# Stick-breaking attention: logits in three 64-row products a head on the two halves of the array, first weights made by VectorE and ScalarE

## The chip, the cores and the metric

The kernel runs on one core of one Trainium2 chip, as one launch. The metric is the device time in microseconds, the median of several executions. One further execution was profiled; all rows quoted here come from its trace.

## The reference, cut to what matters

A two-layer decoder trunk over 1040 tokens (16 learned ones ahead of 1024) and 1024 channels: a Mamba-2 layer with a convolutional FFN, then an attention layer with a second FFN. The change lies in the attention alone, and in the last step ahead of it.

```python
q = (_rmsnorm(h, sb_norm[j]) @ sb_w_q[j]).reshape(b, L, SB_HEADS, SB_HEAD_DIM)   # 16 heads of 64
k_shared, v_shared = split(_rmsnorm(h, kv_norm) @ w_kv)
# for each block of query rows t and key columns s:
logits = jnp.einsum('bthd,bshd->bhts', q, k).astype(jnp.float32) * scale
visible = s_idx < t_idx
log_keep = jnp.where(visible, jax.nn.log_sigmoid(-logits), 0.0)
later = lax.cumsum(log_keep, axis=3, reverse=True) - log_keep
log_w = jnp.where(visible, jax.nn.log_sigmoid(logits) + later, -jnp.inf)
out = jnp.einsum('bhts,bshd->bthd', jnp.exp(log_w), v)
```

All of it is float32, and the logits have to be nearly that exact.

## The kernel before, in words

Activations lie with channels on the partitions and tokens along the free side. Float32 products are made from a high and a low part: `mm3` (L160 to L165) gives high x high, high x low and low x high as three products at the fast rate of the rounded type (`F32R`). The normalised stream `u` is such a pair of tiles for each of eight channel blocks (`KD`); the factor of the RMSNorm for each token is not multiplied in, but lies in `u[KD]` and is applied to what comes out of the products. Tokens are projected in three stretches `TT` of 348, 348 and 344.

At the end of the first FFN, `norm` (L238) is called for each stretch `j`: `parts` splits `h` into `u` (ScalarE copies the high part, VectorE subtracts the low one, L262 and L263), `square_sum` adds the squares (L229, L233, L235), and `rstd` (L190) sums them over the partitions with a product by ones (L196) and makes the factor (L199 to L204). This part is ordered by the scheduler.

The attention (L1414) is in program order on TensorE, VectorE, ScalarE and GpSimd. It works on eight pairs of heads. For each pair, `load` (L1237) fetches the weights of k, q and v (SyncE, L1241), scales them with the norm's gain and splits them into `wh` and `wl`. For the first pair GpSimd scales (L1249) and subtracts (L1254) whole 128x1024 tiles with ScalarE copying between (L1253); for the others VectorE does both in halves (L1260, L1268) with ScalarE's copies between (L1266).

`half` (L1272) does half of one projection (12 products, tile `pj`). When it is whole, a key goes to `key` (L1295), a query to `stack` (L1306). The logits of one head need q.k over 64 channels in the three parts high x high, high x low, low x high. Before, two products of 128 rows do this: the two tiles of `me.ks` and the query's tiles are stacked, so that the 64 rows of the head hold one part and the other 64 rows another. [...] VectorE multiplies the key by the token factor first (L1289), ScalarE takes the high part (L1300, L1313), VectorE the low one (L1301, L1317).

A pair then runs through 18 steps `(i, jj)`: i is one of nine blocks of 116 query rows (112 the last) and jj a stretch of keys, the diagonal one first. In each step, in this order on TensorE: `weigh` (L1351) makes the logits of both heads (L1363, four products into two banks of one tile, 116, 232 or 344 to 348 columns wide), `place` turns projected values (L1330), `half` does its 12 products for the rest of this pair (the first eight steps) or for the next pair (the other ten; the last pair has none there), in every other block `values` (L1394) multiplies weights and values with the two heads in the two halves of the array's columns (L1403), and `turn` (L1379) turns the weights of an earlier step (L1388). ScalarE takes two sigmoids of the logits (L1365), GpSimd masks the diagonal (L1370), VectorE scans (L1374) and multiplies (L1375).

Ahead of the first step stand, in this order, the loads of k, q and v, the projections k, q for the first stretch and k, q for the second (96 products), and `token_factors` (L1337), which turns the token factors of all three stretches (L1345).

Of the kernel before, what the change touches and what calls it, by code (L numbers as in the profile page):

```python
# [8 lines left out]
F32 = mybir.dt.float32  # L9
F32R = mybir.dt.float32r  # L10
AF = mybir.ActivationFunctionType
ALU = mybir.AluOpType

P = 128
D = 1024
KD = D // P
# [7 lines left out]
TW = 352  # L24
QW = 1056
HALO = 4
# [42 lines left out]
class Trunk:  # L69
# [168 lines left out]
    def norm(self, h, j, u):  # L238

        s0, n = TT[j]  # L240
        if u is None:
            u = [(self.Q("uh", F32R), self.Q("ul", F32R)) for _ in range(KD)] + [self.rp.tile([P, QW], F32, tag="r", name=self.nm("r"))]
        rows = [h[k][:, s0 : s0 + n] for k in range(KD)]
        for k in range(KD):
            self.parts(rows[k], u[k], s0, n, None, self.nc.vector)
        self.rstd(self.square_sum(rows, n, D), n, D, u[KD][:, HALO + s0 : HALO + s0 + n], j == 0)
        return u

    def scaled_project(self, w, u, j, q=None, bank=None):
# [977 lines left out]
    def heads(self, u, p, pool):  # L1227


        nc, a = self.nc, self.a  # L1230

        class Pair:
            def __init__(me):
                me.w, me.qd, me.ps = {}, {}, {}
                me.late, me.old = [], []

            def load(me, kind):  # L1237

                src, gain = {"k": (a["w_kv"][p], "kv_norm"), "q": (a["w_q"][p], "sb_norm"), "v": (a["w_kv"][PAIRS + p], "kv_norm")}[kind]
                w32 = self.wp.tile([P, 1024], F32, tag="w32", name=self.nm("w32"))  # L1240
                nc.sync.dma_start(w32, src)  # L1241
                if kind == "k":
                    me.ks = [self.Q("k", F32R), self.Q("k", F32R)]
                elif kind == "v":
                    me.v = pool.tile([P, 9, P], F32, tag="v", name=self.nm("v"), bufs=2)

                def scale():
                    v = w32.rearrange("p (k c) -> p k c", k=KD)
                    nc.gpsimd.tensor_tensor(v, v, self.par(gain, 0, KD).unsqueeze(2).to_broadcast([P, KD, P]), op=ALU.mult)  # L1249

                def parts():
                    me.w[kind] = wh, wl = [self.wp.tile([P, 1024], F32R, tag=t, name=self.nm(t)) for t in ("wh", "wl")]
                    nc.scalar.activation(wh, w32, AF.Copy)  # L1253
                    nc.gpsimd.tensor_tensor(wl, w32, wh.bitcast(F32), op=ALU.subtract)  # L1254

                def scale_halves():
                    for x in range(2):
                        v = w32[:, D // 2 * x : D // 2 * (x + 1)].rearrange("p (k c) -> p k c", c=P)
                        g = self.par(gain, KD // 2 * x, KD // 2).unsqueeze(2).to_broadcast([P, KD // 2, P])
                        nc.vector.tensor_tensor(v, v, g, op=ALU.mult)  # L1260

                def part_halves():
                    me.w[kind] = [self.wp.tile([P, 1024], F32R, tag=t, name=self.nm(t)) for t in ("wh", "wl")]
                    halves = [[t[:, D // 2 * x : D // 2 * (x + 1)] for t in (w32, *me.w[kind])] for x in range(2)]
                    for w, wh, _ in halves:
                        nc.scalar.activation(wh, w, AF.Copy)  # L1266
                    for w, wh, wl in halves:
                        nc.vector.tensor_tensor(wl, w, wh.bitcast(F32), op=ALU.subtract)  # L1268

                return [scale_halves, part_halves] if p else [scale, parts]  # L1270

            def half(me, kind, j, h):  # L1272

                s0, n = TT[j]
                if h == 0:
                    me.ps[kind, j] = self.pj.tile([P, 512], F32, tag="mm", name=self.nm("pj"), bufs=2)
                ps = me.ps[kind, j]
                o, e = HALO + s0, HALO + s0 + n
                wh, wl = me.w[kind]
                for k in range(4 * h, 4 * h + 4):  # L1280
                    self.mm3(ps[:, :n], wh[:, k * P : k * P + P], wl[:, k * P : k * P + P], u[k][0][:, o:e], u[k][1][:, o:e], k == 0, k == KD - 1)
                if h == 0:
                    return []
                del me.ps[kind, j]
                if kind == "q":
                    return [lambda: me.stack(j, ps)]
                t = self.tmp(kind)
                if kind == "k":
                    nc.vector.tensor_tensor(t[:, :n], ps[:, :n], u[KD][:, o:e], op=ALU.mult)  # L1289
                    return [lambda: me.key(j, t)]  # L1290
                nc.scalar.activation(t[:, :n], ps[:, :n], AF.Copy)
                me.late.append((j, t))
                return []

            def key(me, j, t):  # L1295

                s0, n = TT[j]
                c = slice(s0, s0 + n)
                lo, x, y = self.tmp("klo"), *me.ks
                nc.scalar.activation(x[:, c], t[:, :n], AF.Copy)  # L1300
                nc.vector.tensor_tensor(lo[:, :n].bitcast(F32R), t[:, :n], x[:, c].bitcast(F32), op=ALU.subtract)  # L1301
                nc.sync.dma_start(y[64:, c].bitcast(F32), x[64:, c].bitcast(F32))
                nc.sync.dma_start(y[:64, c].bitcast(F32), lo[64:, :n])
                nc.sync.dma_start(x[64:, c].bitcast(F32), lo[:64, :n])

            def stack(me, j, q):  # L1306

                n = TT[j][1]
                out = []
                for a, own in enumerate((slice(0, 64), slice(64, P))):  # L1310
                    t = self.Q("qs", F32R) if j else pool.tile([P, 2 * TW], F32R, tag="qs", name=self.nm("qs"), bufs=2)
                    hi, lo = (t[:, i * TW : i * TW + n] for i in range(2))
                    nc.scalar.activation(hi[own], q[own, :n], AF.Copy)  # L1313
                    out.append((t, hi, lo))
                for a, own in enumerate((slice(0, 64), slice(64, P))):
                    t, hi, lo = out[a]
                    nc.vector.tensor_tensor(lo[own], q[own, :n], hi[own].bitcast(F32), op=ALU.subtract)  # L1317
                    both = t[:, : 2 * TW].bitcast(F32).rearrange("p (i c) -> p i c", i=2)[:, :, :n]
                    nc.sync.dma_start(both[64 - 64 * a : P - 64 * a], both[own])
                me.qd[j] = [x[1:] for x in out]  # L1320

            def place(me):

                todo, me.old, me.late = me.old, me.late, []
                for j, t in todo:
                    v = me.v
                    pv = self.sm("pv")
                    for i in range(3):
                        m = CH[3 * j + i][1]
                        nc.tensor.transpose(pv[:m, i * P : i * P + P], t[:, i * CB : i * CB + m], self.ident)  # L1330
                    for x, y, m in ((0, 3, CB),) if j < 2 else ((0, 2, CB), (2, 3, CH[8][1])):
                        nc.vector.tensor_tensor(v[:m, 3 * j + x : 3 * j + y], pv[:m, x * P : y * P].rearrange("p (c d) -> p c d", d=P),
                                                self.rt[0][:m, 3 * j + x : 3 * j + y].unsqueeze(2).to_broadcast([m, y - x, P]), op=ALU.mult)

        return Pair()
# [15 lines left out]
    def weigh(self, i, jj, qd, ks, prev, pool, ps):  # L1351

        nc = self.nc
        t0, nt = CH[i]
        j, c0 = i // 3, (i % 3) * CB
        s0 = TT[jj][0]
        m = min(TT[jj][1], t0 + nt - s0)
        kp = pool.tile([P, 2, TW], F32, tag="kp", name=self.nm("kp"), bufs=3)
        bt = pool.tile([P, 2, TW], F32, tag="bt", name=self.nm("bt"), bufs=4)
        nc.gpsimd.memset(kp[:nt, :, m : m + 1], 1.0)  # L1360
        for a in range(2):
            for x, part in enumerate(qd[a]):
                nc.tensor.matmul(ps[:nt, a, :m], part[:, c0 : c0 + nt], ks[a][:, s0 : s0 + m], start=x == 0, stop=x == 1)  # L1363
        for t, r in ((kp, self.rt[2]), (bt, self.rt[1])):
            nc.scalar.activation(t[:nt, :, :m], ps[:nt, :, :m], AF.Sigmoid, scale=r[:nt, i : i + 1])  # L1365
        if jj == j:

            for t, fill in ((kp, 1.0), (bt, 0.0)):
                own = t[:nt, :, c0 : c0 + nt]
# [44 lines left out]
    def attention(self, u, pool):  # L1414
# [11 lines left out]
        both = lambda p: p.tile([P, 2, 512], F32, tag="lg2", name=self.nm("lg"))  # L1426
# [20 lines left out]
        for kind, j in (("k", 0), ("q", 0), ("k", 1), ("q", 1)):  # L1447
            for h in range(2):
                for f in first.half(kind, j, h):
                    f()  # L1450
        self.token_factors(u[KD], pool)
        for p in range(PAIRS):
            prev = None
            for n, (i, jj) in enumerate(steps):
# [6 lines left out]
                ps = both(more if p + 1 == PAIRS and n > 8 and n % 2 else self.lp)  # L1461
# [198 lines left out]
```

## Time and profile before

| | |
|---|---|
| median of 3 runs | 2900.92 us (2900.5 to 2902.97) |
| the profiled execution's own time | 2900.43 us |
| its span in the trace | 2898.6 us |
| TensorE busy over the span | 2827.6 us (98%) |
| VectorE, ScalarE, GpSimd | 2111.8, 1642.1 and 674.6 us |
| granted TensorE clock, mean | 0.994 |
| the steps of the attention in the span | from about 1577 to 2093 us |

A row of a timeline reads: start in us from the span's start, its length, the engine (PE is TensorE's product, PEld its weight load, DVE VectorE, ACT ScalarE, POOL GpSimd, SPq SyncE's queue), line, operation, output<-inputs, rows*columns of the array, output's shape, and how many instructions were merged; in brackets the idle time before it and what ended it. A row of a group gives busy time, mean ns, and idle time before. Products are pipelined, so their lengths overlap; their pace is seen from their starts.

### The profile page before, as it was taken

How to read it: one execution, taken by the hardware profiler on the slowest of the kernel's cores; microseconds unless marked ns; L12 is line 12 of the kernel's file. 1: busy time of each engine (PE TensorE's matmuls, PEld its weight loads, DVE VectorE, ACT ScalarE, POOL GpSimd, SP SyncE). 2: the span in 40 equal slices, each digit the busy share in tenths (PEclk: the TensorE clock that was granted, in tenths of full speed). 3: DMA queues.
4: the chain of work that ended last, by engine and by line, in shares of the span. 5: the costliest groups of instructions: out<-in, count | busy, mean ns of one | idle time of the engine just before them, and what ended most of it. 6: DMA issues, size and time to landing. Idle time of an engine off the chain costs nothing.

```text
span 2898.6 us, 55788 instructions
## 1 busy us (share of the span) xinstructions
PE 2827.6 (98%) x21808; PEld 2704.6 (93%) x21808; DVE 2111.8 (73%) x3860; ACT 1642.1 (57%) x3202; POOL 674.6 (23%) x668
## 2 busy tenths in 40 slices
PE   8999999999999999999999999999999999999998
PEld 5989898988999999999998999999898999999888
DVE  5685868776578656568986888888869655657895
ACT  5576667773245555555334777677736555555442
POOL 0000000000004666660002111121101766662000
PEclk9999999999999999999999999999999999999999
DMA  6233333323221222226142222222341222225331
GB/s 168 78 112 86 117 93 108 113 67 136 86 98 66 74 82 76 80 88 214 57 136 77 61 63 63 67 67 56 117 169 46 88 81 81 76 79 189 109 109 59
DMA packets 134135, 274.76 MB, mean 95 GB/s; under 512 B 16464, under 2 KB 68304, under 8 KB 133872
## 3 DMA queue, kind: packets, MB, share of 16 engines
q1 hardware_dynamic: 128560, 260.26, 28.3%
q10 hardware_dynamic: 4048, 6.36, 0.6%
q0 software_dynamic: 1264, 4.57, 0.4%
q8 instruction: 172, 2.82, 0.4%
q14 instruction: 91, 0.75, 0.1%
HBM read 203.02 MB, written 53.21 MB: 88 GB/s over the span
## 4 chain that ended last, share of the span: by engine, by line
PE 70%; DVE 5%; issue 2%; ACT 1%; DMA 1%; POOL 0%; DVEq 0%; ACTq 0%; SPq 0%; POOLq 0%
PE p L163 10%; PE p L165 10%; PE p L164 10%; PE acc L165 8%; PE acc L164 8%; PE acc L163 8%; PE pj L163 3%; PE pj L165 3%; PE pj L164 3%; PE po L1403 2%; PE lg L1363 2%; PE wT L1388 2%; DVE kp L1374 1%; DVE bl L875 1%; DVE ft L879 0%
## 5 line engine op out<-in xcount | busy, mean ns | idle before, releaser
L163 PE MATMUL pj<-uh,wh 128*128 128x348 f32 (+2 forms) x1536 | 502.0, 327 | 10.5 <-DVE xbc L286 9.7
L164 PE MATMUL pj<-ul,wh 128*128 128x348 f32 (+2 forms) x1536 | 494.9, 322 | 0.0
L165 PE MATMUL pj<-uh,wl 128*128 128x348 f32 (+2 forms) x1536 | 493.2, 321 | 0.0
L163 PE MATMUL p<-bh,fh 128*128 128x262 f32 (+1 forms) x1408 | 401.0, 285 | 9.2 <-DVE p L999 4.7
L164 PE MATMUL p<-bl,fh 128*128 128x262 f32 (+1 forms) x1408 | 400.5, 285 | 0.2
L165 PE MATMUL p<-bh,fl 128*128 128x262 f32 (+1 forms) x1408 | 399.3, 284 | 0.0
L163 PEld LDWEIGHTS pj<-uh,wh 128*128 128x128 f32 x1536 | 288.9, 188 | 17.0 <-issue 12.9
L163 PE MATMUL p<-bh,wh 128*128 128x262 f32 (+1 forms) x1056 | 302.3, 286 | 1.2 <-ACT bh L874 1.0
L164 PE MATMUL p<-bl,wh 128*128 128x262 f32 (+1 forms) x1056 | 301.2, 285 | 1.0 <-DVE bl L875 1.0
L165 PE MATMUL p<-bh,wl 128*128 128x262 f32 (+1 forms) x1056 | 302.1, 286 | 0.0
L164 PEld LDWEIGHTS pj<-ul,wh 128*128 128x128 f32 x1536 | 289.4, 188 | 1.5 <-issue 0.6
L165 PEld LDWEIGHTS pj<-uh,wl 128*128 128x128 f32 x1536 | 289.0, 188 | 0.7 <-issue 0.2
L163 PEld LDWEIGHTS p<-bh,fh 128*128 128x128 f32 x1408 | 268.1, 190 | 10.9 <-DVE p L999 5.1
L286 DVE SCALAR_TENSOR_TENSOR c<-p,params,c 128x260 f32<-128x260 f32 (+1 forms) x440 | 207.8, 480 | 91.8 <-ACT c L282 89.8
L164 PEld LDWEIGHTS p<-bl,fh 128*128 128x128 f32 x1408 | 267.6, 190 | 0.8 <-DVE bl L875 0.6
L165 PEld LDWEIGHTS p<-bh,fl 128*128 128x128 f32 x1408 | 266.9, 190 | 0.3
L930 POOL TENSOR_TENSOR fl<-x,fh 128x1024 fp32r<-128x1024 f32 x80 | 192.2, 2403 | 251.7 <-ACT fh L929 251.7
L999 DVE TENSOR_TENSOR p<-p,ft 128x262 f32<-128x262 f32 (+1 forms) x176 | 76.3, 435 | 214.8 <-ACT ft L996 124.4
L164 PE MATMUL acc<-gl,wh 128*128 128x260 f32 (+1 forms) x672 | 211.3, 320 | 0.4 <-DVE gl L1097 0.4
L165 PE MATMUL acc<-gh,wl 128*128 128x260 f32 (+1 forms) x672 | 208.7, 320 | 0.0
L164 PEld LDWEIGHTS p<-bl,wh 128*128 128x128 f32 x1056 | 202.6, 192 | 1.6 <-DVE bl L875 1.6
L163 PEld LDWEIGHTS p<-bh,wh 128*128 128x128 f32 x1056 | 202.5, 192 | 1.7 <-ACT bh L874 1.2
(316 smaller groups left out, 7521.7 us busy)
## 6 DMA issues: line engine op xcount, KB each, us to landing
w<-in_w_up SPq DMA_DIRECT2D x92, 512.0 KB
w<-in_w_down SPq DMA_DIRECT2D x44, 512.0 KB
w<-in_w_in SPq DMA_DIRECT2D x40, 512.0 KB
E<-ea_d SPq DMA_DIRECT2D x32, 464.0 KB
D<-acs_d SPq DMA_DIRECT2D x32, 420.5 KB
g<-c SPq DMA_DIRECT2D x88, 130.0 KB
g<-c SPq DMA_DIRECT2D x88, 128.0 KB
b<-g SPq DMA_DIRECT2D x16, 520.0 KB
```

The source lines that it names most:

```text
L163: mm(out, wh, uh, start=first, stop=False, skip_group_check=joins)
L164: mm(out, wh, ul, start=False, stop=False, skip_group_check=joins)
L165: mm(out, wl, uh, start=False, stop=last, skip_group_check=joins)
L286: nc.vector.scalar_tensor_tensor(to, ps[:, o + i : o + i + n], wcol(i), out, op0=ALU.mult, op1=ALU.add)
L875: tt(hl[1], x, hl[0].bitcast(F32), op=ALU.subtract)
L930: (self.nc.vector if b < 2 else self.nc.gpsimd).tensor_tensor(lo[:, :n], t, hi[:, :n].bitcast(F32), op=ALU.subtract)
L999: add = lambda o, x, y: tt(o[:, :N], x[:, :N], y[:, :N], op=ALU.add)
L1363: nc.tensor.matmul(ps[:nt, a, :m], part[:, c0 : c0 + nt], ks[a][:, s0 : s0 + m], start=x == 0, stop=x == 1)
L1374: nc.vector.tensor_tensor_scan(rev, rev, self.one[:nt].to_broadcast([nt, m + 1]), init, ALU.mult, ALU.mult)
L1388: nc.tensor.transpose(pt[:ns, x * CB : x * CB + nt], bt[a][:nt, x * CB : x * CB + ns], self.ident[:nt, :nt])
L1403: nc.tensor.matmul(po[64 * a : 64 * a + 64, w], v[: CH[c][1], c, 64 * a : 64 * a + 64], wt[a][: CH[c][1], c, :nt], start=x == 0, stop=x == ...
```

## The change

The two heads of a pair lie on partitions 0 to 63 and 64 to 127, in the query as in the key, as the projection leaves them. After the change they stay there: `key` and `stack` make one high and one low tile over all 128 partitions, without copies, and `weigh` makes three products of 64 rows for each head, the heads in turn, so that consecutive products use the upper and the lower 64 rows of the array and write different banks.

Besides, the first pair's weights are made as the other pairs' are, by VectorE and ScalarE in halves, and `norm` keeps the last stretch's `rstd` back; the attention calls it behind the first key and query projections.

```diff
 def norm(self, h, j, u):
-        self.rstd(self.square_sum(rows, n, D), n, D, u[KD][:, HALO + s0 : HALO + s0 + n], j == 0)
+        sums = self.square_sum(rows, n, D)
+        factor = lambda: self.rstd(sums, n, D, u[KD][:, HALO + s0 : HALO + s0 + n], j == 0)
+        if j < 2:
+            factor()
+        else:
+            self.last_factor = factor
 def load(me, kind):
-                def scale():
-                    ...
-                    nc.gpsimd.tensor_tensor(v, v, self.par(gain, 0, KD).unsqueeze(2).to_broadcast([P, KD, P]), op=ALU.mult)
-                def parts():
-                    ...
-                    nc.scalar.activation(wh, w32, AF.Copy)
-                    nc.gpsimd.tensor_tensor(wl, w32, wh.bitcast(F32), op=ALU.subtract)
-                return [scale_halves, part_halves] if p else [scale, parts]
+                return [scale_halves, part_halves]
 def key(me, j, t):
-                lo, x, y = self.tmp("klo"), *me.ks
-                nc.scalar.activation(x[:, c], t[:, :n], AF.Copy)
-                nc.vector.tensor_tensor(lo[:, :n].bitcast(F32R), t[:, :n], x[:, c].bitcast(F32), op=ALU.subtract)
-                nc.sync.dma_start(y[64:, c].bitcast(F32), x[64:, c].bitcast(F32))
-                nc.sync.dma_start(y[:64, c].bitcast(F32), lo[64:, :n])
-                nc.sync.dma_start(x[64:, c].bitcast(F32), lo[:64, :n])
+                hi, lo = (x[:, s0 : s0 + n] for x in me.ks)
+                nc.scalar.activation(hi, t[:, :n], AF.Copy)
+                nc.vector.tensor_tensor(lo, t[:, :n], hi.bitcast(F32), op=ALU.subtract)
 def stack(me, j, q):
-                for a, own in enumerate((slice(0, 64), slice(64, P))):
-                    t = self.Q("qs", F32R) if j else pool.tile([P, 2 * TW], F32R, tag="qs", name=self.nm("qs"), bufs=2)
-                    ...
-                    nc.scalar.activation(hi[own], q[own, :n], AF.Copy)
-                for a, own in enumerate((slice(0, 64), slice(64, P))):
-                    ...
-                    nc.vector.tensor_tensor(lo[own], q[own, :n], hi[own].bitcast(F32), op=ALU.subtract)
-                    nc.sync.dma_start(both[64 - 64 * a : P - 64 * a], both[own])
-                me.qd[j] = [x[1:] for x in out]
+                t = self.Q("qs", F32R)
+                hi, lo = (t[:, i * TW : i * TW + n] for i in range(2))
+                nc.scalar.activation(hi, q[:, :n], AF.Copy)
+                nc.vector.tensor_tensor(lo, q[:, :n], hi.bitcast(F32), op=ALU.subtract)
+                me.qd[j] = hi, lo
 def weigh(self, i, jj, qd, ks, prev, pool, ps):
-        for a in range(2):
-            for x, part in enumerate(qd[a]):
-                nc.tensor.matmul(ps[:nt, a, :m], part[:, c0 : c0 + nt], ks[a][:, s0 : s0 + m], start=x == 0, stop=x == 1)
+        for x, (q, k) in enumerate(((qd[0], ks[0]), (qd[0], ks[1]), (qd[1], ks[0]))):
+            for a in range(2):
+                own = slice(64 * a, 64 * a + 64)
+                nc.tensor.matmul(ps[:nt, a, :m], q[own, c0 : c0 + nt], k[own, s0 : s0 + m], start=x == 0, stop=x == 2)
 def attention(self, u, pool):
+            if (kind, j) == ("q", 0):
+                self.last_factor()
```

More of the change, by code (lines that the diff above doesn't have):

```diff
@@ L1245, in load @@
                     me.v = pool.tile([P, 9, P], F32, tag="v", name=self.nm("v"), bufs=2)
-                def scale():
-                    v = w32.rearrange("p (k c) -> p k c", k=KD)
-                    nc.gpsimd.tensor_tensor(v, v, self.par(gain, 0, KD).unsqueeze(2).to_broadcast([P, KD, P]), op=ALU.mult)
-                def parts():
-                    me.w[kind] = wh, wl = [self.wp.tile([P, 1024], F32R, tag=t, name=self.nm(t)) for t in ("wh", "wl")]
-                    nc.scalar.activation(wh, w32, AF.Copy)
-                    nc.gpsimd.tensor_tensor(wl, w32, wh.bitcast(F32), op=ALU.subtract)
                 def scale_halves():
@@ L1297, in key @@
                 s0, n = TT[j]
-                c = slice(s0, s0 + n)
-                lo, x, y = self.tmp("klo"), *me.ks
-                nc.scalar.activation(x[:, c], t[:, :n], AF.Copy)
-                nc.vector.tensor_tensor(lo[:, :n].bitcast(F32R), t[:, :n], x[:, c].bitcast(F32), op=ALU.subtract)
-                nc.sync.dma_start(y[64:, c].bitcast(F32), x[64:, c].bitcast(F32))
-                nc.sync.dma_start(y[:64, c].bitcast(F32), lo[64:, :n])
-                nc.sync.dma_start(x[64:, c].bitcast(F32), lo[:64, :n])
+                hi, lo = (x[:, s0 : s0 + n] for x in me.ks)
+                nc.scalar.activation(hi, t[:, :n], AF.Copy)
+                nc.vector.tensor_tensor(lo, t[:, :n], hi.bitcast(F32), op=ALU.subtract)
             def stack(me, j, q):
                 n = TT[j][1]
-                out = []
-                for a, own in enumerate((slice(0, 64), slice(64, P))):
-                    t = self.Q("qs", F32R) if j else pool.tile([P, 2 * TW], F32R, tag="qs", name=self.nm("qs"), bufs=2)
-                    hi, lo = (t[:, i * TW : i * TW + n] for i in range(2))
-                    nc.scalar.activation(hi[own], q[own, :n], AF.Copy)
-                    out.append((t, hi, lo))
-                for a, own in enumerate((slice(0, 64), slice(64, P))):
-                    t, hi, lo = out[a]
-                    nc.vector.tensor_tensor(lo[own], q[own, :n], hi[own].bitcast(F32), op=ALU.subtract)
-                    both = t[:, : 2 * TW].bitcast(F32).rearrange("p (i c) -> p i c", i=2)[:, :, :n]
-                    nc.sync.dma_start(both[64 - 64 * a : P - 64 * a], both[own])
-                me.qd[j] = [x[1:] for x in out]
+                t = self.Q("qs", F32R)
[3 more added lines that the diff above has]
+                me.qd[j] = hi, lo
             def place(me):
```

## The prediction

> **What bounds the kernel now.** I read the page first, then busy time by stretches, then the chain of waits, and last the timeline of the two places that the diff touches: the seam before the attention, and one logits group in it.
>
> ```profile
> PE 2827.6 (98%) x21808; PEld 2704.6 (93%) x21808; DVE 2111.8 (73%) x3860; ACT 1642.1 (57%) x3202; POOL 674.6 (23%) x668
> PE 70%; DVE 5%; issue 2%; ACT 1%; DMA 1%; POOL 0%; DVEq 0%; ACTq 0%; SPq 0%; POOLq 0%
> ```
>
> TensorE is nearly always busy and holds 70% of the chain. By stretches (columns: PE, weight loads, DVE, ACT, POOL, then granted clock):
>
> ```profile
> 1554.00:1560.00 6.00, 1.87 (x6) 1.18 (x5) 4.21 (x2) 0.53 (x3) 3.92 (x2) 0.62 0.35 117
> 1618.00:1684.00 66.00, 65.80 (x572) 62.77 (x571) 55.76 (x83) 46.30 (x103) 13.03 (x37) 1.00 0.23 63
> 2057.00:2096.00 39.00, 32.12 (x339) 27.87 (x336) 35.17 (x48) 32.58 (x74) 7.39 (x18) 1.00 0.47 159
> ...
> 1687.41 2.33 PE po L1403 x44
> 1752.96 2.33 PE po L1403 x44
> ```
>
> The last two rows are the same values group (L1403) of neighbouring pairs in the chain: a pair takes 65.55 us, and in it TensorE is busy 65.80 of 66. So in pairs 0 to 6 every ns that a logits group takes on TensorE is a ns of the kernel. Only the last pair, which has no next pair's projections, leaves TensorE about 7 us of slack (32.12 of 39). The seam (1554 to 1560) is the one hole: 1.87 busy of 6, clock down to 0.62.
>
> **Part 1: the logits.** Before, a head's group is two products of 128 rows, four a step for both heads; after, three products of 64 rows a head, six a step. The steps by columns of the moving side:
>
> ```profile
> L1363 PE MATMUL lg<-k,qs x576: 255/321/419, 1576.6 to 2083.6; 128*116 128x348 f32 x80, 128*116 128x116 f32 x48, 128*116 128x232 f32 x32, 128*112 128x344 f32 x16
> L1363 PE MATMUL lg<-k,qs 128*116 128x232 f32 x96 | 16.0, 288 | 0.0
> L1363 PE MATMUL lg<-k,qs 128*116 128x116 f32 x96 | 14.4, 272 | 0.0
> ...
> 1755.40 0.86 PE L1363 MATMUL lg<-k,qs 128*116 128x348 f32 x4
> 1756.10 0.33 PE L163 MATMUL pj<-uh,wh 128*128 128x348 f32 x1
> 1756.27 0.32 PE L164 MATMUL pj<-ul,wh 128*128 128x348 f32 x1
> ...
> 1777.56 0.67 PE L1363 MATMUL lg<-k,qs 128*116 128x232 f32 x4
> 1778.07 0.49 PE L1330 MATMUL pv<-ident,v 128*116 128x128 f32 x3
> ...
> 1783.91 0.60 PE L1363 MATMUL lg<-k,qs 128*116 128x116 f32 x4
> 1784.34 0.52 PE L1330 MATMUL pv<-ident,v 128*116 128x128 f32 x3
> ```
>
> 576 products are 144 steps: 24 with 116 columns, 24 with 232, the other 96 with 344 or 348 (12 of 18 in a pair). Starts, not durations, give the pace, since products overlap: 348 columns come every 0.16 us (1756.10 to 1756.27), so a wide group is 0.64. From its first start to the next product it is 0.70; the middle group is 0.51 and the narrow one 0.43, so these are 0.45 (0.11 each) and 0.37 (0.09 each).
>
> Does a 64-row product run beside the one in the other half? No row here shows it for rows. The nearest is the values product, which alternates between two halves of the columns:
>
> ```profile
> 1642.77 3.13 PE po L1403 x60
> 1636.49 0.60 PE wT L1388 x6
> ```
>
> 60 of them with 116 columns take 3.13 us, 0.052 each; the transposes, 116 columns too but over the whole array, take 0.60/6 = 0.10. So halves do run two at a time, weight loads included. Bounds for six half products: three rounds (0.48, 0.33, 0.27) to six in a row (0.96, 0.66, 0.54). I take three rounds, with the values row. That saves 0.16, 0.11 and 0.09 a group.
>
> What stands against it is the change of the array's shape, twice a step: the transposes ahead of the group and the projections behind it use all 128 rows. The trace has such a visit, a 16-row transpose among whole products, and one to column halves:
>
> ```profile
> 56.65 0.32 PE L165 MATMUL pj<-uh,wl 128*128 128x352 f32 x1
> 56.90 0.13 PEld L323 LDWEIGHTS xT<-ident,x 16*128 16x128 f32 x1 [0.22 <-issue]
> 57.06 0.43 PE L163 MATMUL pj<-uh,wh 128*128 128x352 f32 x1
> 57.16 0.19 PEld L164 LDWEIGHTS pj<-ul,wh 128*128 128x128 f32 x1
> 57.32 0.32 PE L164 MATMUL pj<-ul,wh 128*128 128x352 f32 x1
> ...
> 1773.62 0.32 PE L165 MATMUL pj<-uh,wl 128*128 128x348 f32 x1
> 1773.87 0.62 PE L1403 MATMUL po<-wt,v 116*64 116x116 f32 x8
> ```
>
> Products of this size follow each other at 0.16, yet the 16-row weights start loading only 0.25 later (56.90), and so does the values group (1773.62 to 1773.87): 0.09 of emptying, and the weight load, hidden otherwise, now stands alone (0.10: next load at 57.16 after 57.06). On the way back the same: the whole product's start at 57.06 is 0.26 ahead of the next instead of 0.16, again 0.10 of bare load, behind another 0.05 to 0.09 of emptying. A visit costs 0.09 + 0.10 + 0.08 + 0.10 = 0.37 us. The Trainium skill, "TensorEngine Tiling (Array Packing)", section "Key Properties", says that changing the tiling mode drains TensorE while changing the tile does not; that puts 64-row halves with these rows, which no run here shows for 64 rows. By the doubling that its "Theoretical Speedup" table gives alone, the gaining rival below would be the forecast.
>
> So a group gets longer by 0.37 less the saving: 0.21 wide, 0.26 middle, 0.28 narrow. It counts where TensorE sets the pace: pairs 0 to 6 and the first eight steps of the last pair (they still carry projections; 4 wide, 2 middle, 2 narrow), that is 88 wide, 23 middle, 23 narrow: 18.5 + 6.0 + 6.4 = 30.9 us.
>
> Off that go waits that swallow part of it:
>
> ```profile
>   ACT bt L1365: 1.4, 7
>   PEld pj L163: 2.2, 7
> ...
> L1313 ACT ACTIVATE qs<-pj x48: 439/452/458, 1568.3 to 2054.0; 64x348 fp32r<-64x348 f32 x32, 64x344 fp32r<-64x344 f32 x16
> L1317 DVE TENSOR_TENSOR qs<-pj,qs x48: 500/516/524, 1570.1 to 2056.3; 64x348 fp32r<-64x348 f32 x32, 64x344 fp32r<-64x344 f32 x16
> ```
>
> The first row: before seven logits groups TensorE already waits for ACT to free the bank, 1.4 us together. The second: seven times the projections wait for DVE to finish a query split, 2.2 us; that split shrinks from two instructions of 0.516 to one (all 128 partitions at once), ACT's from two of 0.452 to one, so I take 1.5 of the 2.2 as gone. 30.9 - 1.4 - 1.5 = 28.0. In the last pair's ten later steps TensorE's slack of 7 us covers most of 10 x 0.25; I put 0.5 (0 to 2.5 if the longer group delays the sigmoids). DVE and ACT lose 24 instructions each, some 12 and 10 us in all, and SyncE loses, by the code, six query and nine key copies a pair: no gain, because DVE (55.76 of 66) and ACT (46.30) have slack, and no logits group waits for a copy.
>
> The Trainium skill, "TensorE: Matmul & The Clock Gate", section "Measured speedup vs the span model", gives 3.07 for four 32-row tiles, not 4, which no run here shows. As an estimate, rounds longer by 4/3.07 would add about 0.14 us a wide group and put the kernel near 2940.
>
> **Part 2: the seam.**
>
> ```profile
> 1552.13 0.51 DVE L263 TENSOR_TENSOR ul<-h,uh 128x344 fp32r<-128x344 f32 x1
> 1552.31 1.06 ACT L1253 ACTIVATE wh<-w 128x1024 fp32r<-128x1024 f32 x1
> 1553.44 2.35 POOL L1254 TENSOR_TENSOR wl<-w,wh 128x1024 fp32r<-128x1024 f32 x1 [66.53 <-ACT wh L1253]
> 1554.08 2.09 DVE L263 TENSOR_TENSOR ul<-h,uh 128x344 fp32r<-128x344 f32 x1 [0.56 <-ACT uh L262]
> 1556.09 2.20 DVE L235 TENSOR_TENSOR sq<-sq,sq 128x344 f32<-128x344 f32 x1
> 1558.35 1.52 PE L196 MATMUL ms<-sq,ones 128*128 128x344 f32 x2 [4.13 <-DVE sq L235]
> 1560.24 0.49 PE L164 MATMUL pj<-ul,wh 128*128 128x348 f32 x1
> 1562.42 0.32 PE L163 MATMUL pj<-uh,wh 128*128 128x348 f32 x1
> L1260 DVE TENSOR_TENSOR w<-w,params x42: 681/683/687, 1600.0 to 2013.4; 128x512 f32<-128x512 f32 x42
> L1268 DVE TENSOR_TENSOR wl<-w,wh x42: 678/866/897, 1604.6 to 2017.5; 128x512 fp32r<-128x512 f32 x42
> ```
>
> While GpSimd splits the first weights, the same DVE subtraction takes 2.09 instead of 0.51; TensorE waits 4.13 for the square sum, does the sum's two products, and resumes in a slow clock until 1562.42, the thirteenth projection product. After, GpSimd does none of this, and the last factor comes behind the first 48 products. TensorE then needs DVE's first low half: ACT ends at 1553.37, plus one 0.87, plus perhaps a 0.51 ahead of it, so about 1554.6; the thirteenth product is at about 1556.2. Off the 6.2 gained go the two sums, done later (0.7, an estimate: their 1.52 roughly halved at full clock), and DVE's queue: from 1553.4, six subtractions at 0.87, four scalings at 0.68 (the first two fit earlier) and two old ones, 8.9 us, then the first key's 0.52 before its bank is free at about 1562.9, where TensorE asks for it at 1562.5. Another 0.4 to 0.7. I take -4.5: bounds -6 (nothing late) and -1 (DVE's first scaling falls behind the square sums, and TensorE waits for two more instructions and ACT). The factor's own ACT and DVE steps lie beside the second key and query (48 products, 7.7 us) ahead of the transposes that need them; without that cover they would cost about 3 us. The sums' products wait in TensorE's queue for DVE's square sum, with the second key behind them; the sum is ready at about 1556, TensorE comes to it near 1562.
>
> **Sum.** 28.0 + 0.5 - 4.5 = +24.0 on the profiled 2900.43, which is 0.5 under the median of 2900.92: 2924. Faster or slower here means by more than 0.2% (5.8 us), about what a measurement of this kernel can tell.
>
> **The rivals.**
> (1) *Halves without emptying.* If whole products and 64-row halves follow each other freely, groups get shorter: 88 x 0.16 + 23 x 0.11 + 23 x 0.09 = 18.7, with 1.5 and 4.5 on top: 2876. For it: the values product shows the doubling. Against: its own entry at 1773.87 shows the price. A visit under about 0.19 us decides for this side (134 visits against 18.7 + 1.5 + 4.5).
> (2) *Halves compute together, but their weights load in turn*, 0.10 each: six loads bound the group, +0.39 wide and about +0.54 else: 57.8 after the bank wait, so 2953. Against: the values pace of 0.052 a product with its load.
> (3) *Halves do not run together at all*, the change not doing what it says: +0.69, +0.59, +0.55, less the same waits, 2981. Against: the same row, though it is for columns.
>
> **How the numbers follow.** The forecast 0.70 (own range 2912 to 2936: 0.03 us either way on 134 visits, and the seam's bounds); rival 1 0.10, as both entries speak against it; rival 2 0.09; rival 3 0.07; a visit at about half price, 2896 to 2907, 0.04. The range 2906 to 2955 holds the first and rival 2. Slower 0.86, same 0.03, faster 0.11.
>
> **What would show it.** Right: logits products in pairs a few ns apart, three rounds a group; the first logits load about 0.19 us behind the last transpose's start (0.10 pace, 0.09 emptying), a bare projection load behind the group; a pair of about 69.3 us; at the seam no 4 us hole, no slow clock, DVE subtractions at 0.5 to 0.9. Wrong: a pair under 65 us (rival 1), loads 0.10 apart (2), or 0.16 between halves (3).

## The result, and the profile after

| | median us | against the kernel before (ratio, 95% interval) |
|---|---|---|
| before | 2902.36 (6 runs) | |
| changed | 2917.51 (6 runs) | 1.0055 (1.0044 to 1.0066) |

The change costs 15 us. The profiled execution of the changed kernel took 2919.47, 2 over its median. Its first projection product comes 1.83 us later than in the profile before. Of that, 1.34 stands already ahead of the FFN's last product, where nothing is changed, so times of one place are compared from a start inside that place, not from the span's start. The rest is the change's own, 0.48 by the waits in these rows: VectorE's first weight subtraction (L1264) now stands ahead of the addition that the first projection waits for (the first row is the kernel before, the others the changed one):

```profile
1553.67 0.40 PE L163 MATMUL pj<-uh,wh 128*128 128x348 f32 x1 [0.61 <-DVE h L398]
...
1554.33 0.68 DVE L1264 TENSOR_TENSOR wl<-w,wh 128x512 fp32r<-128x512 f32 x1
1554.93 0.42 DVE L403 TENSOR_TENSOR h<-h,acc 128x260 f32<-128x260 f32 x1
1555.50 0.40 PE L163 MATMUL pj<-uh,wh 128*128 128x348 f32 x1 [1.09 <-DVE h L403]
```

The page, then the stretches (columns as before), then the same values group of neighbouring pairs in the chain:

```profile
PE 2855.0 (98%) x22096; PEld 2691.0 (92%) x22096; DVE 2103.1 (72%) x3848; ACT 1638.6 (56%) x3181; POOL 655.9 (22%) x662
PE 73%; DVE 4%; DMA 1%; ACT 1%; issue 0%; DVEq 0%; ACTq 0%; POOL 0%; SPq 0%
...
1556.00:1562.00 6.00, 6.00 (x40) 6.00 (x39) 5.85 (x11) 2.62 (x5) 0.00 (x0) 1.00 0.57 199
1690.00:1759.00 69.00, 69.00 (x614) 60.71 (x611) 54.61 (x81) 45.48 (x98) 12.07 (x36) 1.00 0.09 32
...
1688.11 2.33 PE po L1389 x44
1756.62 2.33 PE po L1389 x44
```

A pair takes 68.51 us instead of 65.55. TensorE is now busy in all 69 us of it by its records. The hole ahead of the attention is gone (6.00 of 6, full clock). One wide logits group (L1349) among its neighbours, in the timeline:

```profile
1693.37 0.76 PE L1374 MATMUL wT<-ident,bt 116*116 116x116 f32 x6
1694.06 0.73 PE L1349 MATMUL lg<-k,qs 64*116 64x348 f32 x6
1694.73 0.43 PE L163 MATMUL pj<-uh,wh 128*128 128x348 f32 x1
1694.99 0.32 PE L164 MATMUL pj<-ul,wh 128*128 128x348 f32 x1
```

Six products take 0.73 us by their record. In the trace they come in three rounds of two: the two products of a round start 3 ns apart, and so do their weight loads; the second round starts 0.25 behind the first, whose weights load alone, and the third 0.16 behind the second. The six transposes' record ends at 1694.13 and one is 0.26 long, so the last starts at 1693.87, and the logits at 1694.06: 0.19, of which 0.10 is the transposes' pace. Behind the group the projections' first product is 0.26 ahead of the second (0.16 otherwise): the second product's weight load is not hidden. From the last transpose to that second product it is 1.12 us. Before, it was 0.90 (1755.37 to 1756.27), and the logits (1755.40) started 0.03 behind the last transpose, the second of this row:

```profile
1755.22 0.41 PE L1388 MATMUL wT<-ident,bt 116*116 116x116 f32 x2
```

### The profile page after: what moved, and what is told of

The parts are those of the page before. It is cut to its first block, busy times and chain, and to the rows that moved or that the text cites. A ratio compares the mean times of both kernels' runs of the same rounds, so it can differ in the third digit from the quotient of the medians.

```text
span 2917.8 us, 55934 instructions
## 1 busy us (share of the span) xinstructions
PE 2855.0 (98%) x22096; PEld 2691.0 (92%) x22096; DVE 2103.1 (72%) x3848; ACT 1638.6 (56%) x3181; POOL 655.9 (22%) x662
## 4 chain that ended last, share of the span: by engine, by line
PE 73%; DVE 4%; DMA 1%; ACT 1%; issue 0%; DVEq 0%; ACTq 0%; POOL 0%; SPq 0%
PE p L164 10%; PE p L163 10%; PE p L165 10%; PE acc L165 8%; PE acc L164 8%; PE acc L163 8%; PE pj L163 4%; PE pj L165 3%; PE pj L164 3%; PE lg L1349 3%; PE po L1389 3%; PE wT L1374 3%; DVE bl L880 1%; DVE ft L884 0%; DVE c L291 0%
## 5 line engine op out<-in xcount | busy, mean ns | idle before, releaser
L163 PE MATMUL pj<-uh,wh 128*128 128x348 f32 (+2 forms) x1536 | 512.4, 334 | 10.9 <-DVE xbc L291 9.8
L163 PE MATMUL acc<-gh,wh 128*128 128x260 f32 (+1 forms) x672 | 204.3, 320 | 0.0
```

Source lines behind the costliest of these rows:

```text
L163: mm(out, wh, uh, start=first, stop=False, skip_group_check=joins)
```

## The experiments

**The seam alone**, with the logits of before:

```diff
 (before)
-                return [scale_halves, part_halves] if p else [scale, parts]
+                return [scale_halves, part_halves]
-        self.rstd(self.square_sum(rows, n, D), n, D, u[KD][...], j == 0)
+        ...   # kept back for the last stretch, called behind the first key and query, as in the change
```

> The kernel before with the seam alone changed: first weights by VectorE and ScalarE in halves, the last factor behind the first key and query; logits as before (128 rows, stacked by copies). Theory: the hole of 4 us ahead of the attention closes, and TensorE reaches the transposes of the token factors about 6 us sooner after its first projection product (22.0 us in the kernel before, 15.9 in the changed one); all of it counts, as TensorE sets the pace behind it: -5 to -6 us, near 2897. Rival: the time is given back in the first steps, where ScalarE loads a table and the scans start: no change within 2 us.

2897.49 us, ratio 0.9982 (0.9973 to 0.9991): the gain is 5.1 us and stays.

**The logits alone**, with the seam of before:

```diff
 (changed)
-                return [scale_halves, part_halves]
+                return [scale_halves, part_halves] if p else [scale, parts]
-            if (kind, j) == ("q", 0):
-                self.last_factor()
```

> The changed kernel with the old seam (GpSimd makes the first weights, the last factor ahead of the projections): the logits part alone. Theory: +3.0 us a pair as in the changed kernel's trace, +21 in seven pairs and up to 1.7 in the last, so near 2923 to 2925, and the parts add up: seam alone plus this gives the changed kernel within 2 us. Rival: the two parts are not independent (the short query split was needed for the seam, or the reverse), and the sum is off by more than 3 us.

2924.34 us, ratio 1.0077 (1.0065 to 1.0090): +21.7. With the seam's -5.1 that is +16.6, against the +15.2 measured for both: the parts add up.

**Visits alone.** The kernel before, with one nearly empty 64-row product a step:

```diff
 (before, weigh)
+        nc.tensor.matmul(ps[:nt, 0, 400:416], qd[0][0][:64, c0 : c0 + nt], ks[0][:64, s0 : s0 + 16], start=True, stop=True)
         for a in range(2):
             for x, part in enumerate(qd[a]):
```

> The kernel before with one 64-row product of 16 columns, into columns that nothing reads, ahead of each step's logits: a visit to the half shape and back, with hardly any work in it. Theory: emptying and bare weight load twice, 0.33 to 0.39 us a visit, 134 visits where TensorE sets the pace: +44 to +52, less what waits swallow (0 to 6): near 2945. If the waits that are gone in the changed kernel (query split and transposes, 0.85 us a pair) go here too, although the query split is still two instructions, then a slower TensorE removes them, not the shorter split. Rival: visits are cheap and the changed kernel's loss lies elsewhere (bank conflicts, slower 64-row rounds): under +15.

2944.65 us, ratio 1.0146 (1.0131 to 1.0162): +42.0. The timeline of one step (the visit is L1361, the four old products L1364):

```profile
1703.06 0.76 PE L1389 MATMUL wT<-ident,bt 116*116 116x116 f32 x6
1703.75 0.26 PE L1361 MATMUL lg<-k,qs 64*116 64x16 f32 x1
1703.94 0.90 PE L1364 MATMUL lg<-k,qs 128*116 128x348 f32 x4
1704.68 0.32 PE L163 MATMUL pj<-uh,wh 128*128 128x348 f32 x1
```

0.19 from the last transpose to the visit's load, 0.19 from there to the load of the old products, though the visit streams 16 columns: emptying and a bare load, twice. The starts of TensorE's products, added up by what stands ahead of what over six pairs, show where each pair's time lies (us a pair; each cell is the sum of the distances from one start to the next, divided by six; rows that agree in all three are left out):

| from, to | before | changed | visits alone |
|---|---|---|---|
| last transpose to logits | 0.86 | 3.45 | 3.45 to the visit, 3.47 from it |
| within the logits | 8.83 | 6.70 | 9.17 |
| logits to projections or turned values | 2.72 | 4.11 | 2.54 |
| within projections | 31.75 | 33.13 | 31.61 |
| within the turned values (pv) | 0.70 | 0.81 | 0.70 |
| within transposes (wT) | 7.70 | 7.36 | 7.36 |
| a pair | 65.60 | 68.59 | 71.33 |

A visit with next to nothing in it costs 0.37 to 0.38 us: from the last transpose to the second product behind a wide group it is 1.27 instead of 0.90, and the other widths grow alike. By an estimate, about 0.1 of this is the weight load that any further product brings, since transposes of this width follow each other at 0.10; no run here has a whole-height product in the visit's place. Eighteen visits are 6.75 us, but the pair grows by 5.73 (71.33 - 65.60): 1.0 us a pair of waits that TensorE had in the kernel before is gone. They are 0.35 among the transposes, for VectorE's placing of the turned values (L1332); 0.28 behind one wide group, for the query split (L1317); 0.22 ahead of one narrow group, for ScalarE to free the bank; and 0.16 ahead of one wide group, where the profile names no cause. The three rows that the profile before lists for them stand neither in the profile with visits nor in that of the changed kernel:

```profile
PEld pj L163 <- DVE qs L1317: 2.2, 7, 0.3
PEld wT L1388 <- DVE v L1332: 2.1, 6, 0.4
PEld lg L1363 <- ACT bt L1365: 1.4, 7, 0.2
```

(A row gives who waited for whom: us in total, times, the longest.) In the visit run the query split is as long as before. A slower TensorE finds its operands ready; the shorter split is not needed for that.

**The heads not in turn**, three products of one and then three of the other:

```diff
 (changed, weigh)
-        for x, (q, k) in enumerate(((qd[0], ks[0]), (qd[0], ks[1]), (qd[1], ks[0]))):
-            for a in range(2):
-                own = slice(64 * a, 64 * a + 64)
+        for a in range(2):
+            own = slice(64 * a, 64 * a + 64)
+            for x, (q, k) in enumerate(((qd[0], ks[0]), (qd[0], ks[1]), (qd[1], ks[0]))):
```

> The changed kernel with the three products of the first head ahead of the three of the second, so that neighbours lie in the same half of the rows except once in a group. Theory: halves run together only where neighbours differ, so a group needs five rounds instead of three: +0.31 wide, +0.2 middle, +0.2 narrow, in all +36 to +42 over the changed kernel, near 2955. Rival: TensorE looks ahead over three products and pairs them anyway, or the halves never saved anything: no change within 3 us.

2918.39 us, ratio 1.0055 (1.0042 to 1.0069): no difference from the changed kernel. My theory fell. The group looks the same:

```profile
1690.22 0.41 PE L1374 MATMUL wT<-ident,bt 116*116 116x116 f32 x2
1690.56 0.73 PE L1349 MATMUL lg<-k,qs 64*116 64x348 f32 x6
1691.22 0.43 PE L163 MATMUL pj<-uh,wh 128*128 128x348 f32 x1
```

Either the halves keep their own queues, or a 64-row product is short by itself. So the next run took the second half away.

**Both heads in the same half.** The second head gets the first head's logits:

```diff
 (changed, weigh)
-                own = slice(64 * a, 64 * a + 64)
+                own = slice(0, 64)
```

> The changed kernel with all six products of a group on partitions 0 to 63: both heads of a pair get the first head's logits, so the second head's result is left out. What the order of the products did not show is asked here of the half itself. Theory: the halves have queues of their own, and TensorE runs them side by side whatever the order; with one half in use a group needs six rounds: +0.47 wide, +0.33 middle, about +0.3 narrow, +50 to +58 over the changed kernel, near 2971. Rival: a 64-row product simply takes half the time, in whichever half: no change within 3 us.

2974.56 us, ratio 1.0249 (1.0235 to 1.0263): 57 us over the changed kernel.

```profile
1705.38 0.76 PE L1374 MATMUL wT<-ident,bt 116*116 116x116 f32 x6
1706.07 1.20 PE L1349 MATMUL lg<-k,qs 64*116 64x348 f32 x6
1707.20 0.43 PE L163 MATMUL pj<-uh,wh 128*128 128x348 f32 x1
```

1.13 us from the first logits to the projections, 0.67 in the changed kernel: 0.46 for three more rounds. So the halves do run side by side, and with the run before: also when three products of one stand ahead of the other's first.

**Values right behind the logits.**

```diff
 (changed; flush's values part becomes weighted())
                 bt = self.weigh(i, jj, now[0].qd[i // 3], now[0].ks, prev, pool, ps)
+                weighted()
                 todo, late = late, []
```

> The changed kernel with the values product (column halves) moved from behind the projections to right behind the logits, in the five steps of a pair that have one. Theory: what is paid is a change of shape, and rows to columns is one change where it was two (rows to whole, whole to columns): five times 0.2 us a pair, 7 us in all, near 2910. Rival: rows to columns costs as much as both, or the values product now waits for ScalarE's copies of the step before: no gain, or some us slower.

2911.95 us, ratio 1.0033 (1.0020 to 1.0046): 5.6 under the changed kernel, as rows to columns is one change of shape. From the last logits product to the first of the values it is 0.20 us, while in the changed kernel the way leads through the projections, with 0.19 to 0.25 ahead of them and 0.25 behind:

```profile
1682.06 0.76 PE L1374 MATMUL wT<-ident,bt 116*116 116x116 f32 x6
1682.75 0.58 PE L1349 MATMUL lg<-k,qs 64*116 64x232 f32 x6
1683.26 2.40 PE L1389 MATMUL po<-wt,v 116*64 116x116 f32 x44
1685.59 0.42 PE L163 MATMUL pj<-uh,wh 128*128 128x348 f32 x1
```

By the same adding up, a pair falls from 68.59 to 67.85, 0.74 where 1.0 was expected.

**The seam's two halves, each alone**, on the kernel before. The factor alone:

```diff
 (before)
-        self.rstd(self.square_sum(rows, n, D), n, D, u[KD][...], j == 0)
+        ...   # kept back for the last stretch, called behind the first key and query, as in the change
```

> The kernel before with the last factor alone moved behind the first key and query; GpSimd makes the first weights as before. Theory: of the 5 us of the seam most is the wait for the square sum, which stands ahead of the projections; without it TensorE waits only for GpSimd's low weights (until about 1555.8 in the kernel before): -3 to -4, near 2899. Rival: the slow DVE beside GpSimd is what counts; then this gives under 1.5 us.

2900.88 us, ratio 0.9993 (0.9984 to 1.0002): not told from no change, 1.7 us by the medians; neither theory nor rival to the letter. TensorE now waits for GpSimd instead, and DVE is slow beside it as before:

```profile
1554.95 2.36 POOL L1259 TENSOR_TENSOR wl<-w,wh 128x1024 fp32r<-128x1024 f32 x1 [66.33 <-ACT wh L1258]
1555.59 2.09 DVE L268 TENSOR_TENSOR ul<-h,uh 128x344 fp32r<-128x344 f32 x1 [0.56 <-ACT uh L267]
1557.36 0.66 PE L165 MATMUL pj<-uh,wl 128*128 128x348 f32 x1 [1.63 <-POOL wl L1259]
```

The weights alone:

```diff
 (before)
-                return [scale_halves, part_halves] if p else [scale, parts]
+                return [scale_halves, part_halves]
```

> The kernel before with the first weights alone made by VectorE and ScalarE; the last factor stands ahead of the projections. Theory: DVE's two instructions ahead of the square sum go from 2.1 to 0.5 us each, so TensorE's wait falls from 4.1 to about 1 to 2: -2 to -3, near 2900; together with the factor alone more than the 5 us of both, since both shorten the same wait. Rival: DVE's own new work delays the square sum as much: no change.

2896.02 us, ratio 0.9979 (0.9970 to 0.9988): -6.6 instead of -2 to -3, so the seam's whole gain. It is the lowest median of all versions run, but its interval overlaps that of the seam alone (0.9973 to 0.9991). Together with the factor alone it is 8.3, more than the 5.1 of both, as expected (by the distances below 2.4 and 6.1, against 6.2).

```profile
1556.99 0.51 DVE L263 TENSOR_TENSOR ul<-h,uh 128x344 fp32r<-128x344 f32 x1
1557.41 0.51 DVE L235 TENSOR_TENSOR sq<-sq,sq 128x344 f32<-128x344 f32 x1
1559.62 0.74 PE L196 MATMUL ms<-sq,ones 128*128 128x344 f32 x2
```

DVE's two instructions are at 0.51 again, and the sum's products now stand in TensorE's queue behind 26 projection products (1559.62, no wait ahead), where only two stood ahead of them before: the scheduler put them there by itself, though the edit touches only the weights. So this run has both, fast weights and a later sum, and the two are not parted by it. Keeping the factor back by hand as well adds nothing. From the first projection product to the transposes of the factors TensorE takes 22.05 us before, 15.86 in the changed kernel, 15.91 here, 19.65 with the factor alone; where VectorE makes the weights, 0.48 more is lost ahead of that first product, as said above.

**One query split, four copies**, on top of the weights alone:

```diff
-                    nc.scalar.activation(hi[own], q[own, :n], AF.Copy)
-                    ...
-                    nc.sync.dma_start(both[64 - 64 * a : P - 64 * a], both[own])
+                q2 = self.Q("q2", F32R)   # hi, lo over 128 partitions, ScalarE and VectorE once each
+                    for to in (slice(0, 64), slice(64, P)):
+                        nc.sync.dma_start(two(t)[to], two(q2)[own])
```

> The weights alone by VectorE and ScalarE (the seam's whole gain so far), logits of 128 rows as before, and the query split once over all 128 partitions into a tile of its own, from which four copies instead of two fill the stacked tiles. Theory: of the waits that the changed kernel lost, some 0.37 us a pair came from the shorter split, as the visits alone took the others away and left these; TensorE's waits ahead of its projections shrink by that much, and the pair from 65.6 to about 65.2: -2.5 us against the weights alone, near 2893.5. Rival: those waits too go only where TensorE is slower; then no change, or slower by the extra copies.

2922.75 us, ratio 1.0069 (1.0055 to 1.0082), a miss. `q2` took a slot of the ring that the turned weights use, and ScalarE, in order, stood for the copies (DMAs of SyncE) that still read it (the waits):

```profile
ACT wt L1392 <- DMA qs<-q: 30.9, 7, 4.5
```

So once more with a tile of its own:

```diff
-                q2 = self.Q("q2", F32R)
+                q2 = pool.tile([P, 2 * TW], F32R, tag="q2", name=self.nm("q2"), bufs=1)
```

> The same as the one split before it, with the common split in one tile that is set aside for it; the run before took its slot from the ring that the turned weights use, and ScalarE stood 4.4 us seven times for the copies that still read it (30.9 us together). Theory: without that, the pair falls from 65.6 to about 65.2: near 2893.5, 2.5 under the weights alone. Rival: those waits go only where TensorE is slower: no change within 1.5 us.

2904.19 us, ratio 1.0003 (0.9994 to 1.0012), another miss.

```profile
ACT q L1311 <- DMA qs<-q: 13.8, 5, 3.7
PE lg L1363 <- ACT bt L1365: 9.6, 7, 1.4
```

The tile has one buffer; ScalarE waits for the last copies again, 13.8 us over five times, and TensorE 9.6 us for ScalarE. By the same adding up, a pair is 66.40, 0.77 over the weights alone: TensorE waits 1.26 longer ahead of the logits, and 0.36 less behind them and among the projections. Whether the shorter split or the later TensorE saves these 0.36, the run does not show. The premise was wrong too: visits alone had not left 0.37 us of such waits in place. That sum counted three bare loads a pair in the wrong place, and left out the part of the split's wait that stands right behind a logits group; the visits take as much as the changed kernel, 1.0 us a pair.

## Why the prediction was right, and where its sizes were off

2924 was forecast and 2917.5 measured, slower as forecast and within the range of 2906 to 2955. By its steps:

- *Three rounds, halves side by side, weight loads included*: right. The row it was taken from, the values product in column halves, told rightly of row halves: the loads of the two halves start 3 ns apart (against rival 2, loads in turn), and with one half alone the kernel takes 57 us more (against rival 3, halves that do not run together). Rival 2's +0.39 for a wide group is not what six loads of 0.10 give (0.60 - 0.64 + 0.37 = 0.33); nothing rests on it now.
- *A visit of 0.37 us*: 0.37 to 0.38 by the visits alone, where no wait hides part of it. Rival 1, halves without emptying, is out.
- *The groups*: 0.21 wide, 0.26 middle and 0.28 narrow were forecast. From the last transpose to the second product behind the group it is 0.22 wide and 0.27 middle (0.21 where turned values follow), but 0.20 narrow, 70% of what was said: a narrow group's products follow each other at 0.10, as long as a bare weight load takes, and not at 0.09, and the load behind the group stood partly bare before, too. Added up, the groups of a pair cost 4.0 us where 4.1 was forecast.
- *Waits swallowed*: the term that was mis-sized most, 1.0 us a pair where 0.4 was forecast. Of the two waits that were named, the bank's 0.2 went as said, and the query split's 0.28 went whole, not 0.21 of it. Another 0.35 for VectorE's placing of the values and 0.16 ahead of one group were not looked at. The prediction read TensorE's 65.80 busy of 66 as no slack in a pair. The records of products overlap, each about 0.32 long at a pace of 0.16, so short waits do not show in the busy time; they show in the starts. Its reason is not needed either: visits alone free the same waits with the split as it was, and what a shorter split saves by itself no run here shows.
- *Together*: a pair +2.99 instead of about +3.7, seven pairs +20.9, with the last +21.7 (logits alone) instead of +28.5.
- *The seam*: -4.5 forecast, -5.1 measured (seam alone). The mechanism was right in part: GpSimd's weight tiles are what has to go, since they slow VectorE from 0.51 to 2.09 us an instruction, and, with the factor out of the way, come late themselves (1.63). The moved factor adds nothing to that by hand, as the scheduler had moved its products already. That VectorE's own first subtraction would hold up the first projection by 0.48 us was not foreseen.
- *Copies and instructions saved*: no gain was forecast, and the sum of the other terms leaves none to be seen.

The Trainium skill's "TensorEngine Tiling (Array Packing)", section "Key Properties", says that changing the tiling mode drains TensorE; the 0.19 ahead of each group, 0.03 before, agrees. The longer rounds worked out from the Trainium skill's "TensorE: Matmul & The Clock Gate", section "Measured speedup vs the span model", did not come: a round of two takes 0.16 us, as one product of whole height does.

## What to carry to other kernels

Before a product is cut into array halves, count the changes of shape: a visit costs 0.37 us here, more than two wide products, so it has to save more than that in one go; put groups of the same or of another cut shape next to each other (rows to columns is one change), and leave full-height work out of between. Halving the rows while adding products (three for two) saves only a quarter of the group, 0.16 of 0.64. A busy share near 100% does not say that the engine never waits: add up the distances between its starts by what stands ahead of what. And where TensorE idles ahead of a stage, look first at which other engine slows the one it waits for: taking GpSimd's three weight tiles away gave 6.6 us, with a reordering that the scheduler then made by itself, and reordering by hand nothing more.

## What the runs showed that I had not expected

- TensorE runs two row halves side by side although three products of the first stand ahead of the second's first: 2918.39 that way, 2917.51 in turn. The halves need not alternate in the program.
- Slowing TensorE by visits removes 1.0 us a pair of its waits for other engines, so a loss on the bound engine is repaid in part: visits cost 6.75 us a pair and the pair grew by 5.73.
- One VectorE subtraction beside a GpSimd one takes 2.09 instead of 0.51 us, also with the factor out of the way. It ends 0.37 us behind the GpSimd one (1557.68 against 1557.31 in the rows of the factor alone), so it looks as if it stood still until that had ended; no run here shows it apart.
